# A fused two-layer transformer kernel: the spill of the up stage's product goes to ScalarE's DMA queue, and the first loads of the next layer's modulation rows move ahead of the reload of the residual

## The chip, the cores and the metric

The kernel runs on one core of one Trainium2 chip. Five engines with their own instruction streams work side by side: TensorE (PE, the matrix multiplications), VectorE (DVE), ScalarE (ACT), GpSimd (POOL) and SyncE (SP), which in this kernel does nothing but issue DMA transfers. An instruction stream is executed in order: an instruction that waits for a semaphore holds everything behind it on the same engine. The metric is the time of one execution on the device in microseconds, lower is better. Three runs of the kernel before gave a median of 3071.13 us (3068.7 to 3074.3).

## The reference, cut to what matters

The program is two layers (DEPTH = 2) of a hybrid backbone on 1024 latent tokens and 256 context tokens, width 1024, all in float32. Each layer has a mixer (recurrence, global attention, windowed attention), and then a gated feed-forward part with a short convolution over the tokens, which is the part that the change touches:

```python
def conv_ffn(t, w_up, conv_w, conv_b, w_down):
    u = dwconv(t @ w_up, conv_w, conv_b, FFN_PAD[0], FFN_PAD[1])   # 1024 -> 2 x 2816, then 3 taps
    g, v = jnp.split(u, 2, axis=-1)
    return (jax.nn.silu(g) * v) @ w_down                            # 2816 -> 1024

for l in range(DEPTH):
    sh1, sc1, g1, sh2, sc2, g2 = jnp.split(silu(c) @ w_mod[l] + b_mod[l], 6, axis=-1)
    csh1, ... = jnp.split(silu(c_ctx) @ w_mod[l] + b_mod[l], 6, axis=-1)
    ...
    h = h + g2 * conv_ffn(modulate(rms_norm(h, norm2_g[l]), sh2, sc2), w_up[l], ..., w_down[l])
    # the same for the context tokens, in layer 0 only
```

The rows of `w_mod` (1024 x 6144 per layer) are needed for the shifts, scales and gates of a layer. The kernel computes those of layer 1 while layer 0's down projection runs.

## The kernel before, in words

Every float32 product is formed from three products of a rounded "high" part and a "low" remainder (`gemm`): high x high, high x low, low x high. So each weight and each activation has first to be split: ACT copies it into the high part, and POOL (or DVE) subtracts that from the source to give the low part (`split`, lines 308, 322 and 324).

**Up stage** (class `UpProj`). The 2816 hidden columns are handled in 22 slices of 128. A slice needs a weight block for g and one for v. The 1024 latent tokens are not multiplied directly: seven products on half-size sums of weights and activations replace eight (a scheme in Strassen's manner). `part(j, n)` is one of the seven, 12 matmuls of 128x512; the order within a slice is 1, 2, 6, 3, 7, 4, 5. In layer 0 there are also two products for the context tokens (`context`, 24 matmuls of 128x256 each). Parts 6, 3, 7 and 5 use sums of weights: `sums_g(j+1)` loads g a second time, and `sums_v(j+1)` loads v a second time into a buffer that part 3 of slice j reads last (line 151 for all loads), and then forms the sums by four instructions that go DVE, POOL, DVE, POOL (line 178), followed by ACT's and POOL's split. The first product of the next slice that needs the outcome is its part 6, by its third matmul.

At the end of a slice ACT and DVE apply the three taps, ACT the silu, and DVE multiplies g by v (line 254) into the tile `cv` with number 0. From there the slice's product is written to a tensor in DRAM, `y_spill` (line 255). The method `run` calls this store as `self.done()` in the next slice, between part 3 and `sums_v`, so that a slice's store stands ahead of the v load of a later slice on the queue that issues both.

**Down stage** (`down_proj`). `fetch(j)` loads a slice of `y_spill` into `yr` (line 1263) and of `w_down` into `wr` (line 1267) and splits both. `htiles` and line 1315 reload the residual h, which had been written out to make room, in 24 transfers in layer 0. Two slices at a time are multiplied, 6 matmuls for each tile of the output; after each tile one `next(fillers, None)` advances a generator. In layer 0 the generator is `mod_rows(1, ...)`: its first step loads eight blocks of `w_mod` (`mraw`, line 556) into buffers that the up stage's last slices had used, and each later step multiplies one block by the conditioning vectors on DVE (`macc`, lines 570 and 317); after every eight blocks PE sums over the partitions by a product with ones (line 584), DVE copies (line 587), PE transposes (line 314). In layer 1 the generator is empty.

The order within one engine's stream is not that of the source text: a scheduler with priorities of its own places each instruction, so an edit in one place can change the order elsewhere.

Of the kernel before, what the change touches and what calls it, by code (L numbers as in the profile page):

```python
# [29 lines left out]
PC, PL = 2, 260  # L30
# [24 lines left out]
class UpProj:  # L55
# [187 lines left out]
    def conv(self, j, z):  # L243
        b, fc = self.b, self.b.fcol[self.l]
        a0, a1 = (PC if self.cs else PL), PL + SEQ
        t = z * NH + j
        c, r = self.cv[z], self.fr[z]
        b.act(c[:, a0:a1], r[:, a0:a1], AF.Identity, scale=fc[:, 1, t:t + 1], bias=fc[:, 3, t:t + 1])
        b.stt(c[:, a0:a1], r[:, a0 - 1:a1 - 1], fc[:, 0, t:t + 1], c[:, a0:a1], OP.mult, OP.add)
        b.stt(c[:, a0:a1], r[:, a0 + 1:a1 + 1], fc[:, 2, t:t + 1], c[:, a0:a1], OP.mult, OP.add)  # L250
        if z == 0:
            return b.act(c[:, a0:a1], c[:, a0:a1], AF.Silu)
        g = self.cv[0]
        b.nc.vector.tensor_mul(g[:, a0:a1], g[:, a0:a1], c[:, a0:a1])
        self.done = lambda: b.nc.sync.dma_start(b.ysp[j][:, a0 - PC:a1 - PC], g[:, a0:a1])

    def run(self):
        b = self.b
# [33 lines left out]
class Builder:  # L292
# [958 lines left out]
    def down_proj(self, l, chunks, fillers):  # L1251
        nc, io = self.nc, self.io
        cs = "c" in chunks
        a0, a1 = (PC if cs else PL), PL + SEQ
        A, X = self.A0, self.X0
        wspots = (A + 49152, A + 57344, X + 20608, X + 28800, X + 36992, self.W0)
        ys, ws, accs = {}, {}, {}

        def fetch(j):
            o = X + 10304 * (j - 20) if j >= 20 else A + 10304 * (j % 4)  # L1260
            yh, yl = (self.sb("y", [P, PAD], F32R, o + 5152 * q) for q in range(2))
            raw = self.sb("yr", [P, PAD], F32, o + 5152)
            nc.sync.dma_start(raw[:, a0:a1], self.ysp[j][:, a0 - PC:a1 - PC])
            o = A + 65536 + 8192 * (j - 20) if j >= 20 else wspots[j % 6]
            wh, wl = (self.sb("w", [P, D], F32R, o + 4096 * q) for q in range(2))
            wr = self.sb("wr", [P, D], F32, o + 4096)
            nc.sync.dma_start(wr, io["w_down"][l][j * P:(j + 1) * P, :])
            self.split(wh, wl, wr, pool_lo=True)
            self.split(yh[:, a0:a1], yl[:, a0:a1], raw[:, a0:a1])
            ys[j], ws[j] = (yh, yl), (wh, wl)  # L1270

        def term(j, n, ch):
            c0, m = CHUNKS[ch]
            p0 = PC if ch == "c" else PL + c0 - CTX
            (wh, wl), (yh, yl) = ws[j], ys[j]
            return (wh[:, n * P:(n + 1) * P], wl[:, n * P:(n + 1) * P]), (yh[:, p0:p0 + m], yl[:, p0:p0 + m])

        def acc(n, ch):
            if ch == "c":
                o = X + 16384 + 1024 * n if n < 4 else A + 41216 + 1024 * (n - 4)  # L1280
            else:
                o = (A + 65536 if ch == "A" else X) + 2048 * n
            if (n, ch) not in accs:
                accs[n, ch] = self.sb("da", [P, CHUNKS[ch][1]], F32, o)
            return accs[n, ch]

        def group(js, parts, ring, evac):
            for ch in parts:
                c0, m = CHUNKS[ch]
                g = self.mod[l][:, 5, 1 if ch == "c" else 0]  # L1290
                for n in range(KT):
                    ps = self.bank(ring[ch] if isinstance(ring, dict) else ring)[:, :m]
                    self.gemm(ps, [term(j, n, ch) for j in js])
                    evac(n, ch, ps, g[:, n:n + 1], self.h[n][:, c0:c0 + m])
                    next(fillers, None)
                yield ch

        def first(n, ch, ps, g, hv):
            self.act(acc(n, ch), ps, AF.Copy, scale=g)

        def add(n, ch, ps, g, hv):
            self.stt(hv, ps, g, hv, OP.mult, OP.add)

        order = ("A", "B", "c") if cs else ("A", "B")
        fetch(0)
        fetch(1)
        self.h = self.htiles()
        for q in range(0, NH - 2, 2):
            fetch(q + 2)
            fetch(q + 3)  # L1310
            if q == 0:
                for ch in order:
                    c0, m = CHUNKS[ch]
                    for k in range(KT):
                        nc.sync.dma_start(self.h[k][:, c0:c0 + m], self.hsp[k][:, c0:c0 + m])
            for ch in group((q, q + 1), order, (0, 1, 2, 3, 4, 5, 6), first if q == 0 else add):
                if q:
                    continue
                c0, m = CHUNKS[ch]
                for n in range(KT):  # L1320
                    hv = self.h[n][:, c0:c0 + m]
                    eng = nc.vector if ch == "A" else nc.gpsimd
                    eng.tensor_tensor(hv, hv, acc(n, ch), op=OP.add)

        def last(after):
            ring = {ch: (3, 7) if ch == "c" else (0, 1, 2, 3, 7) for ch in CHUNKS}
            for ch in group((NH - 2, NH - 1), order if cs else ("A", "B0", "B1"), ring, add):
                after(ch)
        return last
# [128 lines left out]
```

## Time and profile before

| | |
|---|---|
| median of three runs | 3071.13 us |
| profiled execution, its own time | 3071.41 us |
| its span, first to last instruction | 3069.6 us |
| mean granted clock of TensorE, share of full speed | 0.973 |
| busy: PE / DVE / ACT / POOL | 2847.0 / 2265.6 / 1396.1 / 1226.7 us |
| PE's share of the span | 93% |
| layer 0: up stage, about | 780 to 1360 us |
| layer 0: down stage and modulation rows, about | 1360 to 1960 us |
| layer 1: up stage, about | 2385 to 2800 us |
| layer 1: down stage, about | 2800 to 3069 us |

PE is busy in most of the span, so what counts are its gaps, and stretches in which its granted clock is below full speed. A row of the timeline names the start, the duration, the engine, the line of the code (311 is the matmul inside `gemm`, whoever calls it), the tiles written and read, the shape and the count of instructions merged into the row; a bracket at its end gives the idle time ahead and what ended it.

### The profile page before, as it was taken

To read this page: it belongs to the slowest core of one execution; us is meant where nothing else is said; L and a number is where in the kernel's file an instruction comes from. 1 tells how busy PE (TensorE), PEld (TensorE's weight loads), DVE (VectorE), ACT (ScalarE), POOL (GpSimd) and SP (SyncE) were. 2 spreads that over 40 slices of the span, in tenths; PEclk is the share of its full clock that TensorE was granted. 3 is DMA by queue.
4 is the path that set the end of the run, shared out by engine and by line. 5 is a ranking of instruction groups with operands and counts; after the bars stand their busy time and mean duration, and the time that the engine had idled before them with its cause. 6 is when DMAs were issued, how large, how long until landed. Compare 5 with 4: busy or idle time off the path is not lost. (4 is left out here: it accounts for less than half of the span.)

```text
span 3069.6 us, 38801 instructions
## 1 busy us (share of the span) xinstructions
PE 2847.0 (93%) x14523; PEld 2279.4 (74%) x14523; DVE 2265.6 (74%) x3066; ACT 1396.1 (45%) x2234; POOL 1226.7 (40%) x718
## 2 busy tenths in 40 slices
PE   7999988999999999997999998988999899999998
PEld 4668855678788787876777866966677688887887
DVE  5666898875866666679998766889745987667666
ACT  4675477833433323342111466467753344444114
POOL 1211166542455445544110120147653566665210
PEclk8999999999999999998999999999999999999999
DMA  7423200141333433365354210210022344445221
GB/s 262 139 62 99 68 1 17 39 133 68 97 94 109 108 102 98 93 195 186 110 183 151 83 42 28 61 43 15 21 90 76 96 125 125 127 125 199 84 95 56
DMA packets 295775, 299.56 MB, mean 98 GB/s; under 512 B 16587, under 2 KB 250659, under 8 KB 295587
## 3 DMA queue, kind: packets, MB, share of 16 engines
q1 hardware_dynamic: 295586, 297.09, 31.1%
q8 instruction: 114, 1.87, 0.3%
q14 instruction: 75, 0.61, 0.1%
HBM read 243.02 MB, written 54.02 MB: 97 GB/s over the span
## 5 line engine op out<-in xcount | busy, mean ns | idle before, releaser
L322 POOL TENSOR_TENSOR w<-wr,w 128x1024 fp32r<-128x1024 f32 (+1 forms) x220 | 578.8, 2655 | 474.1 <-ACT w L308 451.3
L311 PE MATMUL bank<-y,w 128*128 128x512 f32 (+1 forms) x2688 | 581.4, 376 | 8.0 <-DVE h L317 5.7
L311 PE MATMUL bank<-xt,w 128*128 128x512 f32 x2112 | 525.8, 402 | 50.4 <-POOL w L322 31.9
L311 PEld LDWEIGHTS bank<-y,w 128*128 128x128 f32 x2688 | 473.1, 193 | 106.7 <-DVE h L317 8.4
L311 PEld LDWEIGHTS bank<-xt,w 128*128 128x128 f32 x2112 | 404.0, 193 | 148.7 <-POOL w L322 40.0
L1061 POOL TENSOR_TENSOR ph<-pf,ph 128x512 fp32r<-128x512 f32 x256 | 339.9, 1349 | 301.7 <-PE bank L311 178.2
L317 DVE SCALAR_TENSOR_TENSOR cv<-fr,fcol,cv 128x1282 f32<-128x1282 f32 (+1 forms) x176 | 375.3, 2189 | 87.9 <-ACT cv L308 87.9
L308 ACT ACTIVATE w<-wr 128x1024 fp32r<-128x1024 f32 (+1 forms) x220 | 223.4, 1016 | 468.7 <-POOL wr L178 346.2
L317 DVE SCALAR_TENSOR_TENSOR h<-bank,mod,h 128x512 f32<-128x512 f32 (+1 forms) x448 | 300.7, 684 | 150.1 <-PE bank L311 149.0
L311 PE MATMUL bank<-a,w 128*128 128x512 f32 x1536 | 388.4, 405 | 10.2 <-ACT a L308 2.4
L311 PE MATMUL bank<-x,w 128*128 128x512 f32 x1584 | 380.8, 391 | 1.8 <-DVE x L317 1.1
L311 PEld LDWEIGHTS bank<-a,w 128*128 128x128 f32 x1536 | 287.0, 190 | 86.5 <-issue 12.4
L311 PEld LDWEIGHTS bank<-x,w 128*128 128x128 f32 x1584 | 297.5, 189 | 64.2 <-issue 1.5
L322 POOL TENSOR_TENSOR w<-raw,w 128x1024 fp32r<-128x1024 f32 x38 | 101.0, 2660 | 428.1 <-ACT w L308 363.8
L311 PE MATMUL bank<-ph,V 128*128 128x512 f32 (+1 forms) x768 | 243.7, 416 | 5.4 <-POOL ph L1061 2.5
L311 PEld LDWEIGHTS bank<-ac,w 128*128 128x128 f32 x1536 | 195.8, 192 | 15.5 <-issue 4.8
L311 PE MATMUL bank<-ac,w 128*128 128x256 f32 x1536 | 204.0, 286 | 2.8 <-ACT lru L308 1.4
L311 PE MATMUL bank<-w,a 128*128 128x256 f32 x1536 | 201.5, 288 | 2.6 <-ACT gq L308 2.6
L311 PEld LDWEIGHTS bank<-w,a 128*128 128x128 f32 x1536 | 191.6, 192 | 10.9 <-issue 6.1
L1003 DVE TENSOR_REDUCE mt<-bank 128x1 f32<-128x512 f32 (+2 forms) x336 | 169.0, 534 | 39.2 <-PE bank L311 36.5
L308 ACT ACTIVATE y<-yr 128x1282 fp32r<-128x1282 f32 (+1 forms) x44 | 51.3, 1168 | 310.4 <-DMA yr<-y_spill 230.8
L311 PE MATMUL bank<-Q,K 128*128 128x512 f32 (+1 forms) x512 | 168.5, 423 | 3.2 <-ACT pf L308 2.9
(205 smaller groups left out, 3849.4 us busy)
## 6 DMA issues: line engine op xcount, KB each, us to landing
wr<-in_w_up SPq DMA_DIRECT2D x154, 512.0 KB
wr<-in_w_down SPq DMA_DIRECT2D x44, 512.0 KB
mraw<-in_w_mod SPq DMA_DIRECT2D x80, 256.0 KB
mraw<-in_w_mod SPq DMA_DIRECT2D x32, 512.0 KB
raw<-in_w_in SPq DMA_DIRECT2D x32, 512.0 KB
y_spill<-cv SPq DMA_DIRECT2D x22, 641.0 KB
yr<-y_spill SPq DMA_DIRECT2D x22, 641.0 KB
y_spill<-cv SPq DMA_DIRECT2D x22, 512.0 KB
```

Source lines behind the costliest of these rows:

```text
L308: return self.nc.scalar.activation(out, in_, func, **kw)
L311: return self.nc.tensor.matmul(out, lhsT, rhs, start=start, stop=stop)
L317: return (eng or self.nc.vector).scalar_tensor_tensor(out, in0, scalar, in1, op0=op0, op1=op1)
L322: self.nc.gpsimd.tensor_tensor(lo, src, hi.bitcast(F32), op=OP.subtract)
L1003: nc.vector.reduce_max(mt[:, 4 * u + s:4 * u + s + 1], ps[:, :n], axis=AX.X)
L1061: nc.gpsimd.tensor_tensor(pl, pf, ph.bitcast(F32), op=OP.subtract)
```

## The change

The store of the up stage's product is issued from ACT's queue in place of SP's, in both layers. In the down stage the generator of the fillers is advanced once between the second `fetch` and the reload of h, so that its first step, the eight loads of `mraw`, comes earlier in the program; each later step comes one output tile earlier.

```diff
@@ -252,7 +252,7 @@
             return b.act(c[:, a0:a1], c[:, a0:a1], AF.Silu)
         g = self.cv[0]
         b.nc.vector.tensor_mul(g[:, a0:a1], g[:, a0:a1], c[:, a0:a1])
-        self.done = lambda: b.nc.sync.dma_start(b.ysp[j][:, a0 - PC:a1 - PC], g[:, a0:a1])
+        self.done = lambda: b.nc.scalar.dma_start(b.ysp[j][:, a0 - PC:a1 - PC], g[:, a0:a1])
 
     def run(self):
         b = self.b
@@ -1304,6 +1304,7 @@
         order = ("A", "B", "c") if cs else ("A", "B")
         fetch(0)
         fetch(1)
+        next(fillers, None)
         self.h = self.htiles()
         for q in range(0, NH - 2, 2):
             fetch(q + 2)
```

From line 1307 on the lines of the changed kernel have numbers one higher. How the scheduler places the instructions is seen on SP first. These are two slices in the middle of layer 0's up stage; `wr` is a weight block, `cv` the slice's product.

```order
 L151 DMA wr_7181<-in_w_up 128x8x128
 L151 DMA wr_7210<-in_w_up 128x8x128
-L255 DMA y_spill<-cv_6443 128x1282
 L151 DMA wr_7354<-in_w_up 128x8x128
 L151 DMA wr_7348<-in_w_up 128x8x128
 L151 DMA wr_7360<-in_w_up 128x8x128
-L255 DMA y_spill<-cv_6443 128x1282
 L151 DMA wr_7389<-in_w_up 128x8x128
```

The stores are gone from SP; behind each of them stood the v load of `sums_v` (`wr_7210`, `wr_7389` are two such loads). On ACT, in the same stage, the store now stands here, behind silu and the copy of the context part, ahead of the splits of the next sums:

```order
 L308 ACTIVATE cv_6443<-cv_6443 128x1282
 L308 ACTIVATE fr_6441<-bank_61 128x256
+L255 DMA y_spill<-cv_6443 128x1282
 L308 ACTIVATE w_7399<-wr_7389 128x1024
 L308 ACTIVATE w_7395<-wr_7360 128x1024
```

On PE, at the start of layer 0's down stage, the first sum over the partitions (line 584) moves ahead by 21 matmuls of the down projection (`y` times `w`), and its transposes (line 314) ahead by some rows:

```order
 L311 MATMUL bank_62<-y_10857,w_10860 128x512
 L311 MATMUL bank_62<-y_10856,w_10861 128x512
+L584 MATMUL bank_65<-macc_10960,ones_7_78 32x128 x4
+L584 MATMUL bank_65<-macc_10961,ones_7_78 32x128 x4
 L311 MATMUL bank_62<-y_10868,w_10872 128x512
 L311 MATMUL bank_62<-y_10869,w_10872 128x512
@@ -5909,10 +5911,8 @@
 L311 MATMUL bank_58<-y_10869,w_10872 128x512
 L311 MATMUL bank_58<-y_10868,w_10873 128x512
-L584 MATMUL bank_65<-macc_10968,ones_7_78 32x128 x4
-L584 MATMUL bank_65<-macc_10969,ones_7_78 32x128 x4
```

Before it, 90 matmuls of the down projection stand in the kernel before and 69 in the changed one. At the start of layer 1's down stage SP's rows are, before the change (`yr_23296` belongs to slice 20, `yr_22208` and `yr_22220` to slices 4 and 5):

```order
L1263 DMA yr_23296<-y_spill 128x1024
L1263 DMA yr_22208<-y_spill 128x1024
L1263 DMA yr_22220<-y_spill 128x1024
L1267 DMA wr_22348<-in_w_down 128x1024
L1267 DMA wr_22360<-in_w_down 128x1024
```

and after it:

```order
L1263 DMA yr_22208<-y_spill 128x1024
L1263 DMA yr_22220<-y_spill 128x1024
L1267 DMA wr_22348<-in_w_down 128x1024
L1267 DMA wr_22360<-in_w_down 128x1024
L1263 DMA yr_23296<-y_spill 128x1024
```

The load for slice 20 has moved behind the four others.

## Rows read from the trace of the kernel before

**Rows 1.** Busy time by engine, TensorE's granted clock, DMA: the two up stages.
```profile
core 0: us, PE busy (x) PEld busy (x) DVE busy (x) ACT busy (x) POOL busy (x), PEclk, DMA share, GB/s
815.00:1330.00 515.00, 488.22 (x2511) 415.45 (x2511) 345.84 (x269) 172.69 (x193) 275.30 (x114) 0.98 0.37 101
2412.00:2780.00 368.00, 367.79 (x1623) 304.54 (x1623) 272.58 (x275) 147.37 (x155) 234.27 (x116) 1.00 0.42 124
```
**Rows 2.** Waits of layer 0's up stage, 815 to 1330: us, times, longest.
```profile
DVE wr L178 <- DMA wr<-in_w_up: 77.8, 18, 5.6
...
PE bank L311 <- POOL w L322: 26.6, 15, 2.8
```
**Rows 3.** Waits of SP's queue over the whole span.
```profile
SPq L255 <- DVE cv L254: 365.2, 44, 15.3
```
**Rows 4.** Timeline of PE, layer 0's up stage.
```profile
843.45 2.91 PE L311 MATMUL bank<-xt,w 128*128 128x512 f32 x12
...
859.98 5.60 PE L311 MATMUL bank<-xt,w 128*128 128x512 f32 x24
...
868.29 2.91 PE L311 MATMUL bank<-xt,w 128*128 128x512 f32 x12
...
881.75 2.57 PE L311 MATMUL bank<-xt,w 128*128 128x512 f32 x10 [1.76 <-POOL w L322]
...
1358.56 2.91 PE L311 MATMUL bank<-xt,w 128*128 128x512 f32 x12
```
**Rows 5.** Timeline of SP's DMA issues, the same slice.
```profile
866.17 0.34 SPq L255 DMA_DIRECT2D y_spill<-cv  x1
...
866.62 0.37 SPq L151 DMA_DIRECT2D wr<-in_w_up  x1
```
**Rows 6.** Timeline of DVE, the same slice.
```profile
864.66 1.48 DVE L254 TENSOR_TENSOR cv<-cv,cv 128x1282 f32<-128x1282 f32 x1
...
866.84 1.29 DVE L218 TENSOR_TENSOR fr<-bank,p 128x512 f32<-128x512 f32 x2
872.78 0.69 DVE L178 TENSOR_TENSOR wr<-wr 128x512 f32<-128x512 f32 x1 [4.65 <-DMA wr<-in_w_up]
...
894.43 1.29 DVE L218 TENSOR_TENSOR fr<-bank,p 128x512 f32<-128x512 f32 x2
900.00 0.69 DVE L178 TENSOR_TENSOR wr<-wr 128x512 f32<-128x512 f32 x1 [4.28 <-DMA wr<-in_w_up]
```
**Rows 7.** Timeline of ACT, the same slice.
```profile
874.93 1.06 ACT L308 ACTIVATE w<-wr 128x1024 fp32r<-128x1024 f32 x1 [10.62 <-POOL wr L178]
```
**Rows 8.** Timeline of DVE, ACT, POOL and PE, layer 1's up stage.
```profile
2520.84 1.21 DVE L254 TENSOR_TENSOR cv<-cv,cv 128x1024 f32<-128x1024 f32 x1
...
2521.15 1.06 ACT L308 ACTIVATE w<-wr 128x1024 fp32r<-128x1024 f32 x1 [0.87 <-DMA wr<-in_w_up]
...
2528.66 6.02 POOL L322 TENSOR_TENSOR w<-wr,w 128x1024 fp32r<-128x1024 f32 x3
...
2536.11 2.88 PE L311 MATMUL bank<-xt,w 128*128 128x512 f32 x12
```
**Rows 9.** Waits of PE, layer 0's down stage, 1360 to 1725.
```profile
PE bank L584 <- DVE macc L317: 32.4, 10, 13.1
```
**Rows 10.** Busy time as in rows 1, start of layer 0's down stage.
```profile
1380.00:1420.00 40.00, 25.64 (x151) 20.84 (x150) 38.35 (x49) 12.88 (x20) 22.84 (x18) 0.83 0.64 211
```
**Rows 11.** Timelines of PE and SP, the same place.
```profile
1398.29 1.08 PE L584 MATMUL bank<-macc,ones 128*32 128x128 f32 x16 [13.08 <-DVE macc L317]
...
1367.58 4.46 SPq L556 DMA_DIRECT2D mraw<-in_w_mod  x8
```
**Rows 12.** Timelines, start of layer 1's down stage: PE, then SP.
```profile
2837.08 25.22 PE L311 MATMUL bank<-y,w 128*128 128x512 f32 x101 [4.57 <-DVE h L317]
...
2822.83 0.33 SPq L1267 DMA_DIRECT2D wr<-in_w_down  x1
2828.98 1.27 SPq L1263 DMA_DIRECT2D yr<-y_spill  x3
```

## The prediction

> **What bounds the kernel now.** I read the busy times by engine first, by stretch, because the change touches two kinds of stage, and then for each stage the wait that ends last on PE. PE is busy in 93% of the span, so a gain can come only from its gaps and from its clock. The two up stages differ [rows 1]: layer 1's has PE busy in 367.79 of 368 us at clock 1.00; in layer 0's 26.8 of 515 us are gaps, and the clock is 0.98. The waits say what the gaps are [rows 2]: 26.6 us in 15 times for POOL's low part of a weight. POOL is no bound (275 of 515 us busy); it is late because DVE, ahead of it in the chain, waits 18 times, 77.8 us in all, for a load of `w_up`.
>
> One slice shows which load and why it is late. Part 3 of the slice ends at 859.98, where PE goes on to parts 7 and 4 [rows 4]; that frees the buffer of the next v load. But SP issues this load only at 866.62, right behind the store at 866.17 [rows 5]; the store waited for the product that DVE begins at 864.66 and needs 1.48 us for [rows 6]. The queue runs in order, so the load stood some 6.5 us behind a store that has nothing to do with it. The load lands at 872.78, where DVE starts on it [rows 6]; the chain from there to the low part ends at 881.75, where PE resumes after 1.76 us [rows 4]. It feeds itself: a late load makes late sums, late sums a late product on DVE, and that a late store, behind which the next load waits again, to land at 900.00 [rows 6]. The loop closes in 900.00 - 872.78 = 27.22 us, while a slice without stall takes PE 868.29 - 843.45 = 24.84 [rows 4].
>
> **Layer 0's up stage: the store leaves SP's queue.** The last part of the slice at 868.29 and that of the last slice at 1358.56 [rows 4] are 18 slices apart: 490.27 us, or 27.24 each. Without stall 18 x 24.84 = 447.1 us. The gain is 43.1 us if nothing else is late: 26.6 us of it are the waits, the rest the slower clock behind them.
>
> What is late next? (1) The load: issued 0.2 us after part 3, at 860.2; landing 6.16 us after its issue as now (872.78 - 866.62; that one had the store beside it), at 866.4. DVE has two additions ahead of it that end at 868.1 [rows 6]. From DVE's start to the low part it takes 881.75 - 872.78 = 8.97 us, so 877.1; needed at 881.75 - 1.76 = 879.99. Slack 2.9 us. (2) DVE: from its first step on the load to its last on the slice 894.43 + 1.29 - 872.78 = 22.94 us, idle time inside included, against 24.84. It fits with 1.9 us left. (3) ACT: the store now stands between silu and the next splits and waits for DVE's product. ACT has nothing to do there: its next split came after 10.62 us of idle time [rows 7]. What the issue costs on ACT no row shows. The nearest is the same issue on SP, 0.34 us [rows 5]; the far end is that ACT were held until a transfer has landed, 6.16 us, which the 10.62 would still cover in layer 0. I take 0.34. So 43.1 us, with 0 and 43.1 as ends: below nothing only by ACT in layer 1, next.
>
> **Layer 1's up stage.** Nothing to gain, PE has no gaps. To lose: ACT's split of the plain v weight starts at 2521.15, and DVE's product ends at 2520.84 + 1.21 = 2522.05 [rows 8]. With the store ahead of it the split waits for that product and the issue, 0.9 + 0.34 = 1.2 us later. Behind it wait POOL's splits, the last three of which end at 2528.66 + 6.02 = 2534.7; PE's part 6 starts at 2536.11 and takes the low part with its third matmul, at 2536.6 [rows 8]. The slack is 1.9 us if it needs the last of the three and 3.9 if the second. I cost it at nothing; if this cover were gone, 22 slices by a microsecond would be 22 us.
>
> **Layer 0's down stage: the early `mraw` loads.** PE waits here 32.4 us in ten times for the partial sums of the modulation rows on DVE, 13.1 of it at once [rows 9], at 1398.29 [rows 11]. The change puts the eighth block's sum ahead of eight additions to h on DVE, but on PE the instruction that needs it also moves ahead, by 21 matmuls. DVE is the bound here: 38.35 of 40 us busy, while PE has 25.64 and its clock is 0.83 [rows 10]. What DVE has to do doesn't get less; so the wait only shrinks by what DVE comes to this place earlier. That is some of the 6.5 us by which its sums of the last slices start earlier against PE. Ends: 13.1 us, the whole first wait; below nothing 4.5 us, because the eight loads take 4.46 us of SP's issue time [rows 11], now ahead of most of the reload of h, whose additions might then be late. I take a gain of 5, near the 6.5.
>
> **Layer 1's down stage.** There the generator is empty, but the scheduler moves SP's loads: those of slices 4 and 5 now stand ahead of slice 20's. PE stalls 4.57 us at 2837.08 [rows 12], and the h additions that end it wait for products of slices whose loads SP issued at 2828.98, 5.8 us after it had become free (2822.83 + 0.33), because slice 20's stood first and waited for its buffer. In the changed order they can go about 6 us earlier, more than the stall. The 101 matmuls behind it take 25.22 us; at the rate of 24 in 5.60 [rows 4] they would take 23.6. Ends 0 and 4.57 + 1.6 = 6.2; I take 5, since the reason for the stall is moved as a whole.
>
> **Sum.** 43.1 + 5 + 5 = 53.1 us off the profiled execution's 3071.41, whose span is 3069.6: 3018.3. The median of the runs, 3071.13, is 0.3 lower: 3018.
>
> **A page that speaks against it.** The Trainium skill, "DMA: Bandwidth & Descriptors", section "Issuing engines are not separate DMA queues", says that transfers of all issuing engines end on the same 16 DMA engines, and that issuing from several "will only save the time on the sequencer it takes to initiate the DMA". By that rule the gain would be the issue time alone; the trace has another cost beside it, the wait in the queue [rows 3], which the sentence does not count.
>
> **The rivals.**
> *Only issue time is saved.* 44 stores of 0.34 us leave SP, 15 us, none of it on PE's path: 3071, no change. For it: most of SP's 365.2 us of waits for the product [rows 3] hold nothing that is due, and in layer 1 the same store holds up nobody. Against it: rows 5 and 6 show the held load and what waits for it. This is what the page's rule comes to. Chance 0.05.
> *DVE's queue takes the wait's place.* If the 22.94 us grow by some 3 us, for instance because DVE and POOL slow each other when they overlap more, the loop closes in about 26 us: 18 x (27.24 - 26) = 22 us, and some 8 of the two transitions: 3041. For it: only 1.9 us are left. Against it: the 22.94 hold 3 to 4 us of waits inside the chain. Chance 0.14.
> *The sums on DVE also come in time.* If all 32.4 us of waits in layer 0's down stage [rows 9] went, or nearly, 23 more than the 5: 2995. Against it: DVE's 38.35 of 40. Chance 0.07.
> *ACT is held by the store (slower).* If an issue keeps ACT for t us, layer 1's split comes 0.9 + t later, and what exceeds a slack of about 3 us falls on PE in each of 22 slices: 22 x (t - 2.1). This eats the gain of 53 at t = 4.5; at 6.16, the time in which a load lands, it is 89 us, which makes 3107. For it: layer 1 has a PE without gaps. Against it: SP's issue takes 0.34, and SP's next instruction follows 0.45 us after the store began [rows 5]. Chance 0.06.
>
> **How the numbers follow.** The forecast as summed has 0.68, from 3006 (both transitions at their better ends, 43 + 13 + 6 = 62, and a little of the further waits) to 3033 (neither transition gains, and 5 us of the loop stay). With the second and the third rival the range is 2994 to 3050; this leaves the first and the last out. A measurement of this kernel can tell about 0.2%, or 6 us, from no change. Faster 0.68 + 0.14 + 0.07 = 0.89; within 0.2% 0.05; slower 0.06.
>
> **What would show it.** In the changed kernel's layer 0 the v load should be issued a fraction of a microsecond after part 3, DVE should wait for another thing than that load, PE's waits for POOL should be gone, the slice take 24.8 to 25 us and the clock be 1.00. If the slice takes 26 and DVE is back to back, the second rival holds. On ACT, the split behind the store should start within half a microsecond of DVE's product; if several microseconds later, the last rival, and PE in layer 1 would have gaps. In layer 0's down stage the wait before the first product with ones should be about 8 us; at 13, that term is nothing. In layer 1's, PE should have no 4.6 us stall. The forecast is wrong if the load still leaves late, held by something else that its buffer or its place in the queue needs.

## The result

The changed kernel takes 3019.5 us in the median of six runs (3014.9 to 3026.5), the kernel before 3070.0 in six runs beside it: ratio 0.984, 95% interval 0.983 to 0.985. The profiled execution is 53.0 us shorter (span 3016.6 against 3069.6), where the working had 53.1. The agreement of the total is partly luck: of the terms one was exact, one too small by 7 us, one had the wrong sign, and one cost that I put at nothing was 2.7 us. By the table below they add up to 43.15 + 12.2 - 0.7 - 2.7 = 52.0 us; 1.8 more come from layer 1's mixer, which the change doesn't touch, and 0.8 are lost outside these stages.

Busy time by engine in the two up stages, with columns as in [rows 1], which the rows answer to:

```profile
815.00:1330.00 515.00, 515.00 (x2732) 445.74 (x2731) 347.43 (x298) 199.71 (x220) 267.49 (x123) 1.00 0.40 125
2350.00:2700.00 350.00, 349.34 (x1528) 286.51 (x1528) 276.80 (x258) 138.62 (x145) 224.80 (x108) 1.00 0.40 123
```

Layer 0's stage is now as layer 1's was: PE has no gap and the full clock. In layer 1's a little is missing, 0.66 us.

The waits, first of layer 0's up stage (800 to 1320; its one PE wait lies before the slices counted below), then PE's of layer 0's down stage (1310 to 1675), for [rows 2] and [rows 9]:

```profile
DVE fr L218 <- PE bank L311: 65.1, 32, 3.7
...
DVE wr L178 <- DMA wr<-in_w_up: 19.6, 18, 1.9
...
PE bank L311 <- POOL w L322: 2.5, 1, 2.5
```

```profile
PE bank L584 <- DVE macc L317: 25.8, 9, 8.8
```

DVE's longest wait is now for PE: who waits for whom has turned round.

One slice, by the timelines of PE, SP, DVE and ACT (for [rows 4] to [rows 7]):

```profile
844.19 2.91 PE L311 MATMUL bank<-xt,w 128*128 128x512 f32 x12
...
860.72 5.60 PE L311 MATMUL bank<-xt,w 128*128 128x512 f32 x24
...
869.03 2.91 PE L311 MATMUL bank<-xt,w 128*128 128x512 f32 x12
...
1316.15 2.91 PE L311 MATMUL bank<-xt,w 128*128 128x512 f32 x12
```

```profile
860.97 0.37 SPq L151 DMA_DIRECT2D wr<-in_w_up  x1
```

```profile
860.20 1.48 DVE L254 TENSOR_TENSOR cv<-cv,cv 128x1282 f32<-128x1282 f32 x1
...
865.38 0.69 DVE L178 TENSOR_TENSOR wr<-wr 128x512 f32<-128x512 f32 x1 [1.05 <-DMA wr<-in_w_up]
```

```profile
861.71 0.33 ACTq L255 DMA_DIRECT2D y_spill<-cv  x1
867.53 1.06 ACT L308 ACTIVATE w<-wr 128x1024 fp32r<-128x1024 f32 x1 [7.67 <-POOL wr L178]
```

Part 3 ends at 860.72, and SP issues the v load 0.25 us later, ahead of the store, which ACT issues at 861.71. DVE starts on the load at 865.38, 4.7 us after part 3, where it was 12.8 us before. ACT still has 7.67 us of idle time ahead of its next split, so the store costs it nothing here.

**The time by stage**, each boundary read from the start of a row in PE's timeline; 18 slices are from part 5 of slice 3 to part 5 of slice 21, a down stage begins with its first matmul of y. The kernels are named as in the experiments.

| kernel | 18 slices, layer 0 | down, layer 0 | mixer, layer 1 | up, layer 1 | down, layer 1 | median |
|---|---|---|---|---|---|---|
| before | 490.27 | 371.57 | 618.05 | 446.30 | 240.57 | 3070.0 |
| changed | 447.12 | 359.37 | 616.21 | 448.96 | 241.28 | 3019.5 |
| store_act | 447.12 | 362.53 | 615.49 | 449.08 | 240.40 | 3018.8 |
| early_mod | 493.54 | 367.74 | 614.27 | 446.34 | 241.64 | 3072.3 |
| vload_act | 447.12 | 361.31 | 617.62 | 446.32 | 241.30 | 3020.1 |
| both_act | 500.52 | 363.03 | 618.20 | 446.29 | 241.86 | 3067.0 |
| act_layer0 | 447.12 | 358.94 | 617.15 | 446.32 | 240.74 | 3015.8 |
| store_pool | 447.12 | 358.82 | 614.49 | 446.31 | 240.35 | 3017.3 |
| best1 | 447.12 | 367.56 | 616.70 | 446.32 | 241.88 | 3023.7 |
| best2 | 447.12 | 361.33 | 618.27 | 446.30 | 244.16 | 3024.8 |
| late_last | 447.12 | 359.97 | 617.01 | 446.35 | 235.63 | 3012.1 |
| sum_later | 447.12 | 349.27 | 615.01 | 446.33 | 243.46 | 3002.8 |
| both_best | 447.12 | 346.99 | 614.52 | 446.31 | 235.25 | 2994.7 |

The medians of the experiments have the kernel before beside them at 3068.6 to 3072.7. The stages are those of one profiled execution each; the mixer, in which none of these kernels differ, shows the scatter: 614.3 to 618.3 us. So a difference of 4 us in a down stage of one execution says little by itself, while the loop's 447.12, the same in ten kernels to the last digit, has no scatter at all: it is PE's bare work.

### The profile page after: what moved, and what is told of

Same layout as the page of the kernel before. It is cut to its first block, busy times and chain, and to the rows that moved or that the text cites. A ratio compares the mean times of both kernels' runs of the same rounds, so it can differ in the third digit from the quotient of the medians.

```text
span 3016.6 us, 38743 instructions
## 1 busy us (share of the span) xinstructions
PE 2827.1 (94%) x14523; PEld 2267.6 (75%) x14523; DVE 2239.6 (74%) x3066; ACT 1399.5 (46%) x2234; POOL 1215.8 (40%) x718
## 5 line engine op out<-in xcount | busy, mean ns | idle before, releaser
L322 POOL TENSOR_TENSOR w<-wr,w 128x1024 fp32r<-128x1024 f32 (+1 forms) x220 | 562.2, 2579 | 386.3 <-ACT w L308 345.9
L311 PE MATMUL bank<-xt,w 128*128 128x512 f32 x2112 | 514.1, 396 | 24.0 <-ACT p L308 8.0
L178 POOL TENSOR_TENSOR wr<-wr,wr 128x512 f32<-128x512 f32 x44 | 57.8, 1313 | 325.0 <-DVE wr L178 193.5
```

Of the source, the lines that this page charges most:

```text
L178: tt = lambda e, out, x, y, op: e.tensor_tensor(out, x, y, op=op)
L311: return self.nc.tensor.matmul(out, lhsT, rhs, start=start, stop=stop)
L322: self.nc.gpsimd.tensor_tensor(lo, src, hi.bitcast(F32), op=OP.subtract)
```

## The experiments

**The two halves of the change, one at a time.** store_act changes line 255 of the kernel before and nothing else; early_mod adds the one call in `down_proj` and nothing else.

```diff
-        self.done = lambda: b.nc.sync.dma_start(b.ysp[j][:, a0 - PC:a1 - PC], g[:, a0:a1])
+        self.done = lambda: b.nc.scalar.dma_start(b.ysp[j][:, a0 - PC:a1 - PC], g[:, a0:a1])
```

Expected of store_act: 

> The store alone is issued from ACT; the modulation rows' first loads stay where they were. My theory (the next v load was held in SP's queue behind a store that waits for DVE's product): layer 0's up stage keeps its whole gain, 490.3 to 447.1 us for 18 slices, and the total is 43 us less plus what of the 12.2 us of layer 0's down stage came with the store: between 3015 and 3027. Rival (the early loads of the modulation rows carry the 12.2 us of the down stage): the total is 12 us above the changed kernel's, about 3031, and PE's wait before the first product with ones is 13 us as before.

Measured: 3018.8 us, ratio 0.983 (0.981 to 0.985). The store alone has the whole gain of the two together: 43.15 us in the loop and 9.0 in layer 0's down stage, less 2.8 in layer 1's up stage.

```diff
         fetch(1)
+        next(fillers, None)
         self.h = self.htiles()
```

Expected of early_mod: 

> The first loads of the modulation rows alone are moved; the store stays on SP. My theory: layer 0's up stage is as before, 27.24 us for a slice, and the down stage gains between 0 and 5 us, since DVE has the same work and sets the pace there: 3065 to 3070. Rival (the early loads are what gave the down stage's 12.2 us): 3058. If PE now asks for the first sum earlier than DVE can give it, the wait grows and the total is up to 5 us above the kernel before, 3075.

Measured: 3072.3 us, ratio 1.000 (0.999 to 1.001). The early loads alone are worth nothing that can be measured. In this execution the down stage is 3.8 us shorter, within the scatter; PE's first wait falls from 13.1 to 9.1 us and the second rises from 1.3 to 5.4.

**Which of the two had to leave SP, and whether a second queue is the point.** vload_act leaves the store on SP and issues the v load of `sums_v` from ACT; both_act issues both from ACT. (`load` gets the engine that issues as a new last argument; that part of the edit is not shown.)

```diff
-        v, oh = self.load(j, 1, 0, 8, o), self.unit()
+        v, oh = self.load(j, 1, 0, 8, o, nc.scalar), self.unit()
```

Expected of vload_act: 

> The store stays on SP, and the v load of the sums is issued from ACT's queue instead; otherwise the kernel before. My theory: what counts is that the load no longer stands behind the store, whichever of the two is moved. A slice of layer 0 takes 24.8 to 25 us, the loop gains 40 to 43, total 3022 to 3030. Rival (the store must leave SP, because while it waits it also holds the loads of the plain weights): the loop keeps a good part of its loss, total 3045 to 3070.

Expected of both_act: 

> The store and the v load of the sums are both issued from ACT's queue, the load right behind the store as it was on SP; otherwise the kernel before. My theory: the load is held again by the store's wait for DVE's product, so the loop keeps its 27 us a slice and the total is 3060 to 3075, or more because ACT's splits now stand behind the held load. Rival (a second queue, or relief of SP's issue time, is what helps): as with the store alone on ACT, 3015 to 3030.

Measured: vload_act 3020.1 us, ratio 0.984 (0.982 to 0.986), loop 447.12. both_act 3067.0 us, ratio 0.999 (0.998 to 1.000), loop 500.52. The pair settles the cause of the loop's loss. In both_act SP is relieved of the stores and 22 loads a layer, and two queues are in use, and no gain shows, since in layer 0 the load again stands behind the store, now on ACT. Its loop is even 10 us longer than that of the kernel before, with 38.9 us of PE's waits for POOL's low parts in place of 26.6; layer 0's down stage, 8.5 us shorter for another reason (see below), makes up for most of it. The timelines of ACT and PE for one slice of both_act:

```profile
1005.18 0.33 ACTq L255 DMA_DIRECT2D y_spill<-cv  x1
1005.60 0.39 ACTq L151 DMA_DIRECT2D wr<-in_w_up  x1
```

```profile
999.92 5.60 PE L311 MATMUL bank<-xt,w 128*128 128x512 f32 x24
```

Part 3 ends at 999.9; the load is issued at 1005.60, right behind the store. It is the picture of [rows 5] on another engine.

**A third queue.** In store_pool the store alone goes to POOL.

```diff
-        self.done = lambda: b.nc.sync.dma_start(b.ysp[j][:, a0 - PC:a1 - PC], g[:, a0:a1])
+        self.done = lambda: b.nc.gpsimd.dma_start(b.ysp[j][:, a0 - PC:a1 - PC], g[:, a0:a1])
```

Expected: 

> The store alone is issued from POOL's queue, in both layers; otherwise the kernel before. My theory: any queue that has nothing due behind the store will do; POOL has its splits and sums behind it, and they belong to the chain that PE waited for, so what POOL loses to the wait for DVE's product and to the issue decides. POOL was idle for 12 us ahead of the sums in layer 0, so the loop keeps its gain: total 3018 to 3030. Rival (POOL's own issue is dear, or the splits stand behind the store): some 1 to 3 us a slice in the two up stages, 3040 to 3110.

Measured: 3017.3 us, ratio 0.983 (0.982 to 0.985). My theory held, with a total a little below its range; POOL's issue takes longer than ACT's but falls into idle time, and layer 1's up stage has its 446.3 us:

```profile
1010.49 0.57 POOL L255 DMA_DIRECT2D y_spill<-cv  x1 [5.12 <-DVE cv L254]
1013.35 1.28 POOL L178 TENSOR_TENSOR wr<-wr,wr 128x512 f32<-128x512 f32 x1 [2.28 <-DVE wr L178]
```

**ACT in layer 0 only.** act_layer0 is the changed kernel with SP's queue again for layer 1's stores.

```diff
-        self.done = lambda: b.nc.scalar.dma_start(...)
+        self.done = lambda: (b.nc.scalar if self.cs else b.nc.sync).dma_start(...)
```

Expected: 

> As the changed kernel, but in layer 1 the store stays on SP. My theory: layer 1's up stage has nothing behind the store that is due, and on ACT the store makes the split of the plain weight wait for DVE's product; back on SP the stage takes 446.3 us as before, not 449.0, and layer 0 is as in the changed kernel: total 2 to 4 us under the changed kernel's, about 3016. Rival (the 2.7 us of layer 1's up stage are scatter of the clock, or come from elsewhere): the stage stays at 449 and the total is the changed kernel's, 3019.5. In layer 1's down stage SP's order is again that of before; both theories expect its stall of 4.6 us.

Measured: 3015.8 us, ratio 0.983 (0.981 to 0.984), layer 1's up stage 446.32. The stage is 449.0 in changed and store_act and 446.3 in all others. The total is 3.7 us under the changed kernel's, which the two intervals, overlapping as they do, would not settle; the stage does. both_act is one of the others, though its store is on ACT in layer 1 too, so it is not the queue that costs 2.7 us but the place: in changed and store_act the store stands ahead of the split of the plain weight, in both_act behind it. ACT's timeline there, changed kernel, then act_layer0, then both_act:

```profile
2465.51 1.06 ACT L308 ACTIVATE cv<-cv 128x1024 f32<-128x1024 f32 x1 [5.49 <-DVE cv L317]
2468.37 0.33 ACTq L255 DMA_DIRECT2D y_spill<-cv  x1
2468.80 1.06 ACT L308 ACTIVATE w<-wr 128x1024 fp32r<-128x1024 f32 x1 [2.23 <-DVE cv L254]
```

```profile
2459.09 1.06 ACT L308 ACTIVATE cv<-cv 128x1024 f32<-128x1024 f32 x1 [3.47 <-DVE cv L317]
2461.07 1.06 ACT L308 ACTIVATE w<-wr 128x1024 fp32r<-128x1024 f32 x1 [0.92 <-DMA wr<-in_w_up]
```

```profile
2523.99 1.06 ACT L308 ACTIVATE w<-wr 128x1024 fp32r<-128x1024 f32 x1 [1.04 <-DMA wr<-in_w_up]
2524.75 0.34 ACTq L255 DMA_DIRECT2D y_spill<-cv  x1
```

From silu to the split it is 3.29 us with the store between, 1.98 without: 1.3 us later, near the 1.2 worked out. What the slack leaves of it is in the next part.

**Less for DVE to do in layer 0's down stage.** best1 is act_layer0 with the eight additions to h of the first 512 tokens on POOL.

```diff
-                    eng = nc.vector if ch == "A" else nc.gpsimd
+                    eng = nc.vector if ch == "A" and not cs else nc.gpsimd
```

Expected: 

> As act_layer0, and in layer 0's down stage the eight additions to h of the first 512 latent tokens go to POOL instead of DVE. My theory: DVE's work sets when the modulation rows' sums are ready; its eight additions took 9.15 us, so PE's first waits (2.9 and 8.8 us) shrink by up to 9 us: total 3007 to 3012. Rival (POOL, which already has the other additions and the splits of the next slices, becomes late and PE waits for its low parts or for h): no gain, or up to 10 us slower than act_layer0, 3016 to 3026.

Measured: 3023.7 us, ratio 0.985 (0.984 to 0.987); the down stage takes 367.56 us, 8.6 more than act_layer0's. My theory failed, and its premise with it: in act_layer0 the eight additions stand behind the first sum's steps on DVE, so taking them away could only help what comes behind it. Instead the first sum on PE comes 4.2 us later after the stage's start (23.3 against 19.1 us). DVE's first two steps for it, which take 0.61 us in act_layer0, now run beside an addition and a split on POOL:

```profile
1329.29 3.80 DVE L570 TENSOR_SCALAR macc<-mraw,cond 128x256 f32<-128x256 f32 x2
```

More on this is in the next part.

**The stall in layer 1's down stage.** best2 is act_layer0 with the y loads of slices 20 and 21 of layer 1 issued from POOL. late_last is act_layer0 with these two tiles laid into buffers that come free only after slices 14 to 17.

```diff
-            nc.sync.dma_start(raw[:, a0:a1], ...)
+            (nc.gpsimd if j >= 20 and not cs else nc.sync).dma_start(raw[:, a0:a1], ...)
```

Expected of best2: 

> As act_layer0, and in layer 1's down stage the loads of slices 20 and 21 of y are issued from POOL's queue, which itself does the additions for which they wait; on SP the loads of slices 4 to 7 no longer have them ahead. My theory for the stall that neither order removed (4.6 us before, 1.8 + 3.3 after): it is the loads of slices 4 to 7 standing behind a load that waits for an addition to h. Then the stall shrinks to under 1 us, layer 1's down stage takes about 236 instead of 240.6 us, total about 3012. Rival (the reload of h holds them, 15 to 24 transfers whose buffers come free late): the stage stays at 240 to 242 us, total 3016.

```diff
-            o = X + 10304 * (j - 20) if j >= 20 else A + 10304 * (j % 4)
+            o = A + 10304 * (j % 4) if j < 20 else X + 10304 * (j - 20) if cs else (X + 20608, self.W0)[j - 20]
```

Expected of late_last: 

> As act_layer0, and in layer 1's down stage the y tiles of slices 20 and 21 lie in buffers that come free only after slices 14 to 17, so that their loads, splits and places on SP, ACT and DVE go to the stage's end. My theory of the stall that stayed in both kernels (4.6 us before, 1.8 + 3.3 after): the loads, ACT's splits or DVE's low parts of slices 4 to 7 stand behind those of slice 20 or 21, which wait for an addition to h, on whichever in-order queue this happens. Then the stall of 4.5 us shrinks to 1 us or less and the stage takes 236 instead of 240.7 us; total 4 us under act_layer0's, about 3012. Rival (the reload of h, the weights of slices 20 and 21 or slices 4 and 5 themselves are late): the stall stays at 3 us or more, the stage at 240 to 242.

Measured: best2 3024.8 us, ratio 0.986 (0.984 to 0.987), the stage 244.16 us, stalls 0.9 and 6.7: worse (only 3.4 of the 9 us above act_layer0 lie in this stage). late_last 3012.1 us, ratio 0.981 (0.979 to 0.983), the stage 235.63, one stall of 1.23. SP's order with the loads of slices 4 to 7 ahead was the same in both. In best2 SP issues the loads of slices 4 and 5 at 2771.60, but POOL issues the first of slices 20 and 21 only behind its additions, and ACT begins the next splits of y only after that one:

```profile
2777.57 0.70 POOL L1263 DMA_DIRECT2D yr<-y_spill  x1 [0.31 <-POOL h L1324]
```

```profile
2782.34 2.95 ACT L308 ACTIVATE y<-yr 128x1024 fp32r<-128x1024 f32 x3 [5.86 <-DMA yr<-y_spill]
```

I read the three splits of this row as slice 20's, which kept its place, and those of slices 4 and 5 behind it. Only when loads, splits and low parts of slices 20 and 21 all went to the end did the stall go.

**PE asks later for the sums.** sum_later is act_layer0 with two more output tiles between the last `macc` of a block and its product with ones; both_best has this and the buffers of late_last.

```diff
-        rest = (3, 3) if lag else (2, 1)
+        rest = (5, 3) if lag else (2, 1)
```

Expected of sum_later: 

> As act_layer0, and in layer 0's down stage PE asks for each sum over the partitions two output tiles later (rest 5 in place of 3). My theory: DVE falls behind only where it has other work at once, and over the whole stage has time left; then PE's waits for the sums, 19.6 to 25.8 us, shrink to under 8 and layer 0's down stage takes 345 to 350 instead of 359 us: total 3002 to 3010. Rival (DVE is the bound of the whole stage, so a later request only moves the wait, or the last sums come so late that the next layer waits): total within 3 us of act_layer0's 3016, or above it.

Expected of both_best: 

> late_last and sum_later together. If both theories hold the gains add, 4 + 10: total 2998 to 3006. If one of them fails, the total is that of the other.

Measured: sum_later 3002.8 us, ratio 0.978 (0.976 to 0.980); the stage takes 349.27. PE's waits there:

```profile
PE bank L314 <- DVE ms L587: 14.6, 5, 6.8
PE bank L584 <- DVE macc L317: 2.7, 6, 0.9
```

In act_layer0 the second is 19.6 us and the first 4.6, so most of the waits for the sums are gone, and waits for the copy of the sums (line 587) have taken the place of part of them; something more is to be had there. both_best 2994.7 us, ratio 0.976 (0.974 to 0.978), the fastest kernel here, 0.8% faster than the changed one.

## Why the prediction was right, and where it was not

*The loop of layer 0's up stage* (43.1 us, measured 43.15). Every step to the gain held: the load 0.25 us after part 3, no PE wait, clock 1.00, 24.84 us a slice. both_act shows the cause, vload_act and store_pool that it doesn't matter who steps aside. The 18 slices, before and changed (columns as in [rows 1]):

```profile
868.29:1358.56 490.27, 463.38 (x2378) 393.60 (x2377) 326.31 (x252) 165.59 (x183) 258.47 (x108) 0.98 0.39 107
869.03:1316.15 447.12, 447.12 (x2378) 387.36 (x2377) 297.60 (x253) 169.31 (x184) 232.16 (x108) 1.00 0.38 120
```

PE's idle time was 26.9 us, and the same matmuls took 16.3 us longer before. The clock in the row, 0.98, makes some 9 us of these (an estimate, 2% of 463.38); what the others are, the rows don't show. The second rival had the sign wrong: DVE's time for the same work did not grow but fell, from 326.3 to 297.6 us, so the 26 us a slice never came. (Its 3 to 4 us of waits inside the chain were 4.7, idle times of 1.46 and 3.27 us in DVE's rows of that slice.)

*Only issue time is saved* (a chance of 0.05, 3071). The sentence quoted from the Trainium skill, "DMA: Bandwidth & Descriptors", section "Issuing engines are not separate DMA queues", counts the issue time alone, and both_act agrees with it: two queues in place of one gave nothing clear of the noise (0.998 to 1.000). But the store waited for a product; what is saved is the time that the queue stood, which the sentence leaves out, and that was worth 43 us.

*Layer 0's down stage* (a gain of 5, measured 12.2 in the profiled pair; 12.6 in act_layer0, 9.0 in store_act). Two things in this term failed.

First, it counted only PE's waits for the sums and put everything else at nothing. The whole stage before, changed, in vload_act and in both_act (columns as in [rows 1]):

```profile
1361.31:1732.88 371.57, 335.13 (x1772) 273.05 (x1771) 329.75 (x527) 78.30 (x90) 81.78 (x43) 0.95 0.49 161
1318.90:1678.27 359.37, 332.13 (x1772) 270.40 (x1771) 319.96 (x524) 74.99 (x86) 83.26 (x42) 0.96 0.49 159
1319.57:1680.88 361.31, 331.91 (x1772) 270.99 (x1770) 322.30 (x523) 75.36 (x86) 78.48 (x42) 0.96 0.49 159
1372.55:1735.58 363.03, 331.56 (x1771) 269.58 (x1770) 324.44 (x525) 74.22 (x86) 84.64 (x43) 0.96 0.49 161
```

Of the 12.2 us, 9.2 are PE's idle time, and 3.0 are the same 1772 matmuls, run at a mean granted clock of 0.96 in place of 0.95. The waits for the sums give 6.6 of the 9.2 (32.4 to 25.8), which is near the 5; two waits at the stage's start (0.57 for ACT's and 1.71 for POOL's part of a weight before, none after) give 2.3. Inside the 6.6 the first wait shrank to 2.9 us, not to the 8 forecast, and the second grew from 1.3 to 8.8.

Second, the step that DVE, as the bound, has the same work, so that the wait shrinks only by what DVE comes to it earlier. The count is the same, the time is not. DVE's rows from the last slice's taps to the additions, before and changed; the two rows of `macc` before (12 and 2) answer to one after (14):

```profile
1368.71 8.16 DVE L317 SCALAR_TENSOR_TENSOR cv<-fr,fcol,cv 128x1282 f32<-128x1282 f32 x4 [1.02 <-ACT cv L308]
...
1378.73 10.03 DVE L317 SCALAR_TENSOR_TENSOR macc<-mraw,cond,macc 128x256 f32<-128x256 f32 x12
1388.68 9.15 DVE L1323 TENSOR_TENSOR h<-h,da 128x512 f32<-128x512 f32 x8
1397.76 0.87 DVE L317 SCALAR_TENSOR_TENSOR macc<-mraw,cond,macc 128x256 f32<-128x256 f32 x2
```

```profile
1322.77 5.95 DVE L317 SCALAR_TENSOR_TENSOR cv<-fr,fcol,cv 128x1282 f32<-128x1282 f32 x4 [0.99 <-ACT cv L308]
...
1330.56 7.77 DVE L317 SCALAR_TENSOR_TENSOR macc<-mraw,cond,macc 128x256 f32<-128x256 f32 x14
1338.26 4.89 DVE L1324 TENSOR_TENSOR h<-h,da 128x512 f32<-128x512 f32 x8
```

The four taps took 8.16 us before and 5.95 after, the 14 steps 10.9 and 7.8, the eight additions 9.15 and 4.89: 28.2 against 18.6 us for the same instructions. (The additions also went behind the first sum, as forecast.) What differs is POOL beside them. While the eight additions ran, POOL did four of its own before, and after one, which took 7.63 us where one before took 1.3 to 1.7:

```profile
1389.17 6.31 POOL L1323 TENSOR_TENSOR h<-h,da 128x512 f32<-128x512 f32 x4 [1.49 <-DMA h<-h_spill]
```

```profile
1336.67 7.63 POOL L1324 TENSOR_TENSOR h<-h,da 128x512 f32<-128x512 f32 x1 [2.98 <-DMA h<-h_spill]
```

So one of the two engines stands while the other works, as I read these rows, and which one was settled anew by the moved loads. best1 points the same way: with eight additions moved from DVE to POOL, DVE's first two steps on `macc` took 3.80 us in place of 0.61. The Trainium skill, "SBUF — State Buffer", section "Who interferes with whom", says that a DVE instruction with two inputs in SBUF contends with a POOL instruction that reads SBUF, and that the ports they share are an exclusive lock; the additions agree, both kinds having two inputs in SBUF, though POOL's one addition stood through a run of DVE's and not through one.

What this is worth is another question, and two runs answer it. both_act has the shorter rows alone: its loop is as late as before, DVE's taps begin 6.77 us after the stage's first matmul (7.40 before), the same instructions take 22.7 us, the additions 4.89, and the stage is 8.5 us shorter. vload_act has the earlier start alone, the step of the prediction: DVE's taps begin 2.64 us after the stage's first matmul, and the same instructions take 27.2 us, almost as before:

```profile
1331.19 10.10 DVE L317 SCALAR_TENSOR_TENSOR macc<-mraw,cond,macc 128x256 f32<-128x256 f32 x12
1341.21 9.15 DVE L1323 TENSOR_TENSOR h<-h,da 128x512 f32<-128x512 f32 x8
```

Its stage is 10.3 us shorter. So even with the scatter of some 4 us in mind, neither the shorter rows nor the earlier start is needed for most of the gain, and the step was wrong in its "only". The changed kernel has both (3.87 us, 18.6 us) and does not gain the sum of 8.5 and 10.3; how its 12.2 us divide between them is not shown. Nor is DVE the bound of the whole stage, which the prediction took from a stretch of 40 us: in sum_later PE asks later, DVE has the same to do, and the waits for the sums all but go. The third rival, that they would all go by this change, did not come: 25.8 of 32.4 us stayed.

*Layer 1's down stage* (a gain of 5, measured a loss of 0.7). The step that failed is that the loads of slices 4 and 5, once ahead of slice 20's, would take the stall with them. They did go earlier. PE's and SP's timelines of the changed kernel, for [rows 12]:

```profile
2773.34 15.77 PE L311 MATMUL bank<-y,w 128*128 128x512 f32 x66 [1.84 <-ACT da L308]
2792.41 22.82 PE L311 MATMUL bank<-y,w 128*128 128x512 f32 x91 [3.30 <-DVE h L317]
```

```profile
2766.83 2.85 SPq L1267 DMA_DIRECT2D wr<-in_w_down  x2
2769.78 0.86 SPq L1263 DMA_DIRECT2D yr<-y_spill  x2
2770.73 0.98 SPq L1267 DMA_DIRECT2D wr<-in_w_down  x2
2779.11 16.15 SPq L1263 DMA_DIRECT2D yr<-y_spill  x4
```

Counted from the stage's first matmul (2797.23 and 2743.44) the loads of slices 4 and 5 went at 26.3 us, where the row that holds them began at 31.8 before. But the weight of slice 20 or 21, issued at 17.7 us before, stood behind all of the reload of h and went at 23.4; ACT's split of it, the first row here, stood ahead of ACT's drains of the banks, and PE waited 1.84 us for those. And the four y loads at 2779.11 begin with slice 20's, ahead of slices 6 and 7; a low part on DVE that waits for the split of such a late slice, the second row, stands ahead of DVE's drains, for which PE waited 3.30 us:

```profile
2771.65 1.06 ACT L308 ACTIVATE w<-wr 128x1024 fp32r<-128x1024 f32 x1 [8.61 <-DMA wr<-in_w_down]
```

```profile
2789.57 2.12 DVE L324 TENSOR_TENSOR y<-yr,y 128x1024 fp32r<-128x1024 f32 x1 [2.89 <-ACT y L308]
```

The stall had moved on by two slices. late_last shows that the place of slices 20 and 21 is the cause (both_best, 8.2 us shorter in this stage than sum_later, shows it again), and best2 that SP's order is only one of three in-order queues in which it sits.

*Layer 1's up stage* (nothing, with 22 slices by a microsecond if the cover were gone; measured a loss of 2.7). The delay was right (1.3 us against 1.2). The step that failed is the slack of 1.9 us, read from one slice: it does not cover the delay in every slice, and 0.12 us a slice remain on average, mostly as 0.2 us at a time in PE's part 6 of some slices (3.1 us for 12 matmuls that take 2.88). The slower rival, ACT held by its issue, did not come: ACT's issue takes 0.33 us, and the split follows 0.43 us after it began.

## What to carry to other kernels

Look in each queue that issues DMAs for an instruction that waits for a late producer, and at what stands behind it; a wait that is harmless by itself (of SP's 365 us of waits for the product only some 6.5 us a slice of layer 0 held a load that was due) costs the time that it holds the thing behind it where that thing heads a chain that closes on the producer. Here moving either of the two to another queue, where nothing due stood behind it, gave the same gain, and moving both together none. When a prediction takes an order of loads as the reason for a stall, follow the late slice through all in-order engines (load, split, low part), since the same order sits in each. And don't carry DVE's durations from one profile over to a schedule in which POOL works beside it at other times.

## What was not expected of the hardware

DVE and POOL slowed each other far more than the load on either suggests: one addition of 128x512 on POOL took 1.3 to 1.7 us before and 7.63 beside DVE's additions after, and a step of DVE that takes 0.35 us in the median took up to 2.57 us, beside a POOL split, in the kernel before. In layer 0's loop one of DVE's taps of 128x1282 took 2.87 us in the median before and 1.55 in the changed kernel. A store issued from POOL held it 0.57 us, from ACT 0.33, from SP 0.34.
